# A pass that puts products of ones into TensorE's order where a replay of the plan sees it wait

## The chip, the cores and the metric

The kernel runs on one core of one Trainium2 chip. The metric is the device time of one execution in microseconds (us), as the median of several runs. The engines are named as in the profile: PE (TensorE, its products) and PEld (its weight loads), DVE (VectorE), ACT (ScalarE), POOL (GpSimd), SP (SyncE, which issues all transfers here).

## The reference

Two layers of a streaming encoder for 512 prompt positions and 64 sample positions, all in float32, width 1024:

```python
def trunk_layer(x, conv_state, k_past, v_past, ki_past, ...):
    a, g, q, k, v, qi, ki, wi = jnp.split(x @ w_in, points, axis=-1)
    u = a * jax.nn.sigmoid(g)
    conv_out, new_conv = conv_mixer(u, conv_state, conv_w, conv_b, cln_g, cln_b)   # 31 taps, layer norm, silu
    ...                                                                            # rope of q, k, qi, ki
    attn_out = dsa_attention(q, k_all, v_all, qi, ki_all, wi, pos, topk)           # indexer picks topk keys
    mix = jnp.concatenate([conv_out, attn_out], axis=-1) @ w_o
    x = layer_norm(ALPHA * x + mix, ln1_g, ln1_b)
    gate, up = jnp.split(x @ w_gate_up, 2, axis=-1)
    ffn = (jax.nn.silu(gate) * up) @ w_down
    x = layer_norm(ALPHA * x + ffn, ln2_g, ln2_b)
    return x, k, v, ki, new_conv
```

## The kernel before

Positions lie along the free dimension (576 columns, in two halves of 288), features on the 128 partitions. Each operand of the large products is split into a high and a low float32r part, and a product is made of three float32r products (`XH,whi`, `XH,wlo`, `XL,whi`). The small products (convolution, attention values, sums for the layer norms) are float32.

Nothing is issued while the program is being written down. Every call goes to a `Plan`, which records an operation with its views, its priority and a price per engine (`price`, from line 217). At the end `schedule` lays all operations out in time with those prices, engine by engine, by priority and readiness, with transfers and buffer places; the order that comes out is issued to the five queues by `issue` (line 352; all instructions carry line 362 for that reason). Each queue then runs strictly in that order on the chip, and what a wait really costs the plan does not know. Prices are, for instance, 0.069 us + n/960 for a DVE operation on n columns, 0.06 us + n/1200 (+ 0.035 outside PSUM) for ACT, 0.15 us + 0.0021 n for POOL.

The stages of a layer, twice over: the input products with rope and the indexer (to about 110 us of layer 1), the selection of keys on DVE and the convolution (64 x 5 products per layer, whose tap matrices `taps` POOL makes from `eyes` and `wv`), attention in blocks 0 to 4 (`logits` with products `qk`, `values` with transposes `pp` and products `po`), the convolution's layer norm (`conv_sums`, `Moments.stats`, `Moments.spread`), the output products, layer norm 1 (`Sums`), then the gated FFN in four parts as products of halves (`Seven`, products `q`, `r`, `c`) and the down products, layer norm 2.

One PSUM tile of two banks, tag `w` (function `wide`), is shared in turn by the convolution's accumulators (`conv`), `stats`, `spread`, `cshift` and the logits of attention block 4. It was shaped `[P, 2, 512]`. A convolution group is five products that accumulate in one stretch of its columns; the products of other work may stand between them in PE's order.

Of the kernel before, what the change touches and what calls it, by code (L numbers as in the profile page):

```python
# [11 lines left out]
F32 = mybir.dt.float32  # L12
F32R = mybir.dt.float32r
# [43 lines left out]
UW = PH * CIN  # L57
CWID = PH * COUT

O_CB, O_CG, O_CBE = 0, NCT * PH, NCT * PH + NCT  # L60
# [110 lines left out]
TABLES = {AF.Exp: "exp", AF.Silu: "silu", AF.Sigmoid: "sigmoid", AF.Sqrt: "sqrt"}  # L171
HOP, TABLE_LOAD, TABLE_LEAD = 0.2, 1.283, 0


class Plan:
# [77 lines left out]
    def schedule(self):  # L253
# [96 lines left out]
        return order  # L350

    def issue(self):
        nc = self.tc.nc
        take = lambda v: v.real() if isinstance(v, View) else v
        with self.tc.manual_schedule():
            for op in self.schedule():
                for t in op.tiles.values():
                    if t.ap is None:
                        tag = f"{t.tag}.{t.place}"
                        t.ap = t.pool.tile(t.shape, t.dt, tag=tag, name=t.name, bufs=1)  # L360
                engine = getattr(nc, op.done[2])
                getattr(engine, op.method)(*map(take, op.args), **{k: take(v) for k, v in op.kw.items()})  # L362
# [3 lines left out]
def stream_step(ctx, tc, ins, outs):  # L366
# [44 lines left out]
    def wide(name):  # L411
        return pw.tile([P, 2, 512], F32, tag="w", name=name)

# [75 lines left out]
    class Moments:  # L489
# [5 lines left out]
        def stats(self):  # L495
            m, tiles, count = self.m, self.tiles, self.count
            ps = wide("stats")
            for b, c in ((0, 496), (1, 504)):
                for i in range(tiles):
                    nc.tensor.matmul(ps[:m, 0, c + i:c + i + 1], self.s[b][:, i * m:(i + 1) * m], ones[:, 0:1],  # L500
                                     start=True, stop=True)
# [3 lines left out]
            nc.vector.tensor_scalar(nmu, ps[:m, 0, 496:496 + tiles], -1.0 / count, None, op0=OP.mult)  # L505
            nc.vector.tensor_mul(msq, nmu, nmu)
            nc.vector.scalar_tensor_tensor(rstd, ps[:m, 0, 504:504 + tiles], 1.0 / count, msq,
                                           op0=OP.mult, op1=OP.subtract)
            nc.vector.tensor_scalar(rstd, rstd, 0.0, LN_EPS, op0=OP.max, op1=OP.add)
            nc.scalar.activation(rstd, rstd, AF.Sqrt)  # L510
            nc.vector.reciprocal(rstd, rstd)

        def spread(self, b):

            m, tiles, n, dst = self.m, self.tiles, self.n, self.dst[b]
            per = tiles if tiles == 3 else tiles // 2
            ps = wide("spread")
            for i in range(tiles):
                nc.tensor.matmul(ps[:, i // per, (i % per) * m:(i % per + 1) * m],
                                 self.st[:m, b, i:i + 1].to_broadcast([m, P]), ident[:m, :m], start=True, stop=True)  # L520
# [122 lines left out]
    def layer(l):  # L643
# [10 lines left out]
        def convolve(c):  # L654
# [8 lines left out]
            for b in range(PH):  # L663
# [3 lines left out]
                                     wv[:, b, :].unsqueeze(2).to_broadcast(shape))  # L667
                o = b % 4 * COUT
                for j in range(CJ):
                    nc.tensor.matmul(ps[:, b // 4, o:o + COUT], sw[:, j * P:(j + 1) * P], v[:, b, j:j + COUT],  # L670
                                     start=(j == 0), stop=(j == CJ - 1))
            y = slot.tile([P, PH, COUT], F32, tag=f"u{c}", name=f"y{c}")
            for h in range(2):
                nc.vector.tensor_add(y[:, 4 * h:4 * h + 4, :], ps[:, h, :4 * COUT].rearrange("p (b t) -> p b t", b=4),
                                     prm[0][:, O_CB + c * PH + 4 * h:O_CB + c * PH + 4 * h + 4].unsqueeze(2)
# [11 lines left out]
        def conv_sums():  # L687
# [5 lines left out]
            for c in range(4):  # L693
                acc = cs[c]
                if c == 0:
                    shift = slot.tile([P, UW], F32, tag="u0", name="cshift")[:, :CWID]
                    ps = wide("cshift")
                    for h in range(2):
                        nc.tensor.matmul(ps[:, h, :CWID // 2], ones, acc[:, h * CWID // 2:(h + 1) * CWID // 2],
                                         start=True, stop=True)  # L700
# [213 lines left out]
        def logits(t, u):  # L914
# [13 lines left out]
            else:  # L928
                g = u // 2
                ps = wide("qk").rearrange("p a b -> p (a b)")  # L930
                q = qsm[:, u * P:(u + 1) * P]
# [395 lines left out]
```

## Time and profile before

| | |
|---|---|
| median of 3 runs | 1520.78 us (1516.83 to 1522.31) |
| the profiled execution: device time | 1524.12 us |
| its span from first to last instruction | 1522.4 us |
| its mean granted TensorE clock | 0.939 |
| busy: PE / DVE / ACT / POOL | 1449.1 / 1104.6 / 721.4 / 496.0 us |

All rows are from the one profiled execution. [...] A matmul's end is modelled, so PE can be called busy throughout a stretch in which its products merely follow each other more slowly; the spacing from start to start tells the real rate.

### The profile page before, as it was taken

The numbers are of one execution on the slowest core, as the hardware profiler recorded it, in microseconds if no ns is written. First come the engines' busy times: TensorE is split into PE (matmuls) and PEld (weight loads), VectorE is DVE, ScalarE is ACT, GpSimd is POOL, SyncE is SP. The second block draws the span as 40 slices with busy tenths as digits, with TensorE's granted clock in tenths as the row PEclk, the third lists the DMA queues.
The fourth block names the chain that finished last, engine by engine and source line by source line (L and its number), as shares of the span: only waits on it lengthen the run. The fifth ranks groups of instructions, "written<-read, shape, count | busy, mean of one in ns | idle before, by whom it ended". The sixth has DMA issues, their size and how long they took to land.

```text
span 1522.4 us, 26598 instructions
## 1 busy us (share of the span) xinstructions
PE 1449.1 (95%) x10246; PEld 1413.3 (93%) x10246; DVE 1104.6 (73%) x2040; ACT 721.4 (47%) x1421; POOL 496.0 (33%) x437
## 2 busy tenths in 40 slices
PE   6999999998999999999998998999899999999996
PEld 6889897997999999999998998889889999999996
DVE  3679886468678577587768997855596875865875
ACT  4444445645446245265444434465363552543643
POOL 2322554243113123033614245633420230320342
PEclk9989787898999999999999995959999999999997
DMA  5614220011222322223234241101112222222221
GB/s 201 188 52 119 54 70 17 29 56 56 77 104 78 103 89 92 84 98 103 69 102 125 86 125 52 45 14 42 56 50 88 99 94 87 94 91 81 80 74 63
DMA packets 66207, 125.12 MB, mean 82 GB/s; under 512 B 27936, under 2 KB 34208, under 8 KB 66080
## 3 DMA queue, kind: packets, MB, share of 16 engines
q1 hardware_dynamic: 66080, 123.42, 25.3%
q8 instruction: 80, 1.31, 0.4%
q14 instruction: 47, 0.39, 0.1%
HBM read 108.81 MB, written 9.21 MB: 78 GB/s over the span
## 4 chain that ended last, share of the span: by engine, by line
PE 78%; DVE 13%; ACT 3%; issue 2%; DMA 2%; POOL 1%; SPq 1%; ACTq 0%; DVEq 0%; POOLq 0%
PE prod L362 33%; PE q L362 16%; PE r L362 8%; PE conv L362 5%; PE c L362 4%; PE po L362 3%; DVE X L362 2%; DVE sel L362 2%; DVE rope_h L362 2%; PE qk L362 2%; PE dots L362 2%; PE pp L362 2%; PE spread L362 2%; DVE wlo L362 2%; PE stats L362 1%
## 5 line engine op out<-in xcount | busy, mean ns | idle before, releaser
L362 DVE TENSOR_TENSOR wlo<-raw,whi 128x512 fp32r<-128x512 f32 (+2 forms) x199 | 246.2, 1239 | 90.8 <-ACT whi L362 88.7
L362 ACT ACTIVATE whi<-raw 128x1024 fp32r<-128x1024 f32 (+2 forms) x206 | 182.9, 889 | 254.5 <-PE prod L362 179.1
L362 PE MATMUL prod<-XH,whi 128*128 128x288 f32 (+2 forms) x928 | 282.9, 310 | 18.5 <-ACT whi L362 16.4
L362 PE MATMUL prod<-XH,wlo 128*128 128x288 f32 (+2 forms) x928 | 285.0, 310 | 7.4 <-DVE wlo L362 7.4
L362 PE MATMUL prod<-XL,whi 128*128 128x288 f32 (+2 forms) x928 | 285.9, 310 | 2.9 <-DVE XL L362 2.8
L362 PE MATMUL prod<-hl,whi 128*128 128x288 f32 x704 | 208.1, 296 | 0.7 <-DVE hl L362 0.5
L362 PE MATMUL prod<-hh,wlo 128*128 128x288 f32 x704 | 207.8, 296 | 0.0
L362 PE MATMUL prod<-hh,whi 128*128 128x288 f32 x704 | 207.0, 295 | 0.0
L362 PEld LDWEIGHTS prod<-XH,whi 128*128 128x128 f32 (+1 forms) x928 | 177.6, 193 | 22.5 <-ACT whi L362 17.3
L362 PEld LDWEIGHTS prod<-XH,wlo 128*128 128x128 f32 (+1 forms) x928 | 177.9, 192 | 10.4 <-DVE wlo L362 8.3
L362 PEld LDWEIGHTS prod<-XL,whi 128*128 128x128 f32 (+1 forms) x928 | 178.9, 193 | 7.7 <-DVE XL L362 5.8
L362 ACT ACTIVATE whi<-s 128x512 fp32r<-128x512 f32 x160 | 96.4, 626 | 134.9 <-PE q L362 102.0
L362 DVE TENSOR_TENSOR wlo<-s,whi 128x512 fp32r<-128x512 f32 x158 | 107.7, 703 | 63.5 <-ACT whi L362 62.5
L362 PE MATMUL q<-XH,wlo 128*128 128x288 f32 x480 | 141.2, 296 | 1.5 <-DVE wlo L362 1.3
L362 PE MATMUL q<-XL,whi 128*128 128x288 f32 x480 | 141.4, 295 | 0.0
L362 PE MATMUL q<-XH,whi 128*128 128x288 f32 x480 | 141.3, 295 | 0.0
L362 PEld LDWEIGHTS prod<-hl,whi 128*128 128x128 f32 x704 | 132.1, 188 | 1.8 <-DVE hl L362 1.4
L362 PEld LDWEIGHTS prod<-hh,wlo 128*128 128x128 f32 x704 | 132.0, 188 | 0.1
L362 PEld LDWEIGHTS prod<-hh,whi 128*128 128x128 f32 x704 | 131.9, 188 | 0.2
L362 POOL TENSOR_TENSOR s<-raw 128x512 f32<-128x512 f32 x28 | 45.0, 1611 | 247.8 <-DVE wlo L362 209.7
L362 DVE TENSOR_TENSOR X<-X,prod 128x288 f32<-128x288 f32 x120 | 53.4, 451 | 86.8 <-PE prod L362 86.1
L362 POOL TENSOR_TENSOR taps<-eyes,wv 128x640 f32<-128x640 f32 x64 | 86.9, 1361 | 71.0 <-PE conv L362 57.2
(197 smaller groups left out, 3560.1 us busy)
## 6 DMA issues: line engine op xcount, KB each, us to landing
raw<-in_w_u SPq DMA_DIRECT2D x44, 512.0 KB, 3.2
raw<-in_w_g SPq DMA_DIRECT2D x44, 512.0 KB, 3.2
raw<-in_w_in SPq DMA_DIRECT2D x36, 512.0 KB, 3.9
raw<-in_w_d SPq DMA_DIRECT2D x48, 384.0 KB, 3.0
raw<-in_w_o SPq DMA_DIRECT2D x16, 512.0 KB, 3.3
raw<-in_w_d SPq DMA_DIRECT2D x16, 256.0 KB, 2.6
rope_s<-rope_h SPq DMA_DIRECT2D x48, 72.0 KB, 2.0
ud<-u SPq DMA_DIRECT2D x8, 320.0 KB, 2.9
```

The source lines that it names most:

```text
L362: getattr(engine, op.method)(*map(take, op.args), **{k: take(v) for k, v in op.kw.items()})
```

## The change

A new pass `filled` takes the order that `schedule` gave and replays it: five queues in order, the same prices with some corrections (a port that DVE and POOL hold in turn, a table load, transfers at 300 GB/s with 1.2 us at the end, `spacing` for the products, always at the full clock). Where the replay finds PE waiting by `t - now`, it puts `int(0.9 * wait / 0.237)` markers ahead of the waiting operation. `issue` turns a marker into a float32 product of the tile of ones with itself, 128 x 128 by 128 columns, into columns 816 to 943 of the `w` tile that was last opened, which nothing else uses. While an accumulation group of a `w` tile is open, markers are held back (`due`) until it is closed. For the first product the wait counts from 1.0 us on. The condition with `FORCE` never holds, since `FORCE` is 0.

The `w` tile becomes `[P, 1024]`, so that its columns can be cut as one range; for that, the copies out of the `spread` of the convolution's norm and out of `cshift` are two activations of 304 columns instead of one of 608. Everything else computes what it did.

```diff
+WB = CWID // 2
...
+SIGNAL, IDLE, FILL, CLOCK, FORCE, LATE = 0.04, (0.237, 0.213), 0.9, 3.4, 0.0, 1
...
+    def filled(self, order):
+
+        free, ended, held, out = dict.fromkeys(("tensor", "vector", "scalar", "gpsimd", "sync"), 0.0), {}, {}, []
+        dma, table, port, recent, act, begun = 0.0, None, ["", 0.0], [], 0.0, False
+        for op in order:
+            e = op.done[2]
+            t = free[e]
+            for w in op.waits:
+                if w.done[2] != e:
+                    t = max(t, ended[w.seq] + SIGNAL)
+                elif e != "tensor":
+                    t = max(t, ended[w.seq] + 0.02)
...
+            if op.method == "dma_start":
+                free[e] = t + op.generate
+                dma = max(dma, free[e] + 0.65) + op.nbytes / 300e3
+                end = dma + 1.2
+            elif e == "tensor":
+                cost, streamed = self.spacing(op)
+                now = free[e]
+                if not begun:
+                    now, begun = 1.0, True
+                n = int(FILL * (t - now) / IDLE[0])
+                while recent and recent[0][0] < now - CLOCK:
+                    act -= recent.pop(0)[1]
+                if act < FORCE * CLOCK and n < LATE:
+                    n += 1
+                for _ in range(n):
+                    out.append(None)
+                    recent.append((now, IDLE[1]))
+                    act += IDLE[1]
+                    now += IDLE[0]
+                t = max(t, now)
+                recent.append((t, streamed))
+                act += streamed
+                free[e] = t + cost
+                end = free[e] + 0.18
...
+    def spacing(self, op):
+
+        n = op.args[0].columns()
+        if op.method == "transpose":
+            return 0.111, n / 2400
+        if n == 1:
+            return 0.16, 0.0
+        if F32R in (op.args[1].tile.dt, op.args[2].tile.dt):
+            return max(0.111, 0.0065 + 0.0004375 * n), n / 2400
+        return 2 * max(0.111, 0.0065 + 0.000875 * n), n / 600
+
     def issue(self):
         nc = self.tc.nc
         take = lambda v: v.real() if isinstance(v, View) else v
         with self.tc.manual_schedule():
-            for op in self.schedule():
+            t, cols, ones = self.filler
+            idle, due, group = t.pool.tile(t.shape, t.dt, tag=f"{t.tag}.0", name=t.name, bufs=1), 0, set()
+            for op in self.filled(self.schedule()):
+                if op is None:
+                    due += 1
+                while due and not group:
+                    nc.tensor.matmul(idle[:, cols], take(ones), take(ones), start=True, stop=True)
+                    due -= 1
+                if op is None:
+                    continue
+                if op.method == "matmul" and op.args[0].tile.tag == self.filler[0].tag:
+                    (group.discard if op.kw["stop"] else group.add)(op.args[0].idx.flat[0])
...
     def wide(name):
-        return pw.tile([P, 2, 512], F32, tag="w", name=name)
+        return pw.tile([P, 1024], F32, tag="w", name=name)
...
     nc.gpsimd.memset(ones, 1.0)
+    nc.filler = Held(pw.pool, [P, 1024], F32, "w", "idle", 1), slice(512 + WB, 512 + WB + P), ones
...
-            if tiles > per:
-                nc.scalar.activation(dst.rearrange("p (a b) -> p a b", a=2), ps[:, :, :n // 2], AF.Copy)
-            else:
-                nc.scalar.activation(dst, ps[:, 0, :n], AF.Copy)
+                o = 512 * (i // per) + i % per * m
+                nc.tensor.matmul(ps[:, o:o + m], self.st[:m, b, i:i + 1].to_broadcast([m, P]), ident[:m, :m], start=True, stop=True)
+            for a in range(0, n, per * m):
+                nc.scalar.activation(dst[:, a:a + per * m], ps[:, a // (per * m) * 512:][:, :per * m], AF.Copy)
...
-                    nc.scalar.activation(shift.rearrange("p (a b) -> p a b", a=2), ps[:, :, :CWID // 2], AF.Copy,
-                                         scale=-1.0 / P)
+                    for h in range(2):
+                        nc.scalar.activation(shift[:, h * WB:(h + 1) * WB], ps[:, 512 * h:512 * h + WB], AF.Copy,
+                                             scale=-1.0 / P)
```

## Rows read from the trace of the kernel before

**Rows 1.** From the page: busy time of each engine, and the granted clock of TensorE in 40 equal slices (9 is 0.9 or more).

```profile
PE 1449.1 (95%) x10246; PEld 1413.3 (93%) x10246; DVE 1104.6 (73%) x2040; ACT 721.4 (47%) x1421; POOL 496.0 (33%) x437
...
PEclk9989787898999999999999995959999999999997
```

**Rows 2.** The windows view, all engines: stretch (us from the start of the span) and its length; then busy us and number of instructions of PE, PEld, DVE, ACT and POOL; then the granted clock, the DMA share and GB/s.

```profile
76.00:79.00 3.00, 1.00 (x9) 0.99 (x10) 2.77 (x6) 0.32 (x1) 0.63 (x1) 1.00 0.05 10
79.00:89.40 10.40, 10.40 (x49) 10.40 (x49) 6.00 (x10) 2.29 (x6) 5.46 (x4) 0.51 0.01 3
166.00:171.30 5.30, 2.67 (x23) 2.54 (x22) 5.21 (x14) 3.00 (x5) 2.58 (x3) 1.00 0.35 113
171.30:198.50 27.20, 26.64 (x122) 25.64 (x123) 19.81 (x53) 11.87 (x37) 16.28 (x17) 0.50 0.15 42
199.00:238.00 39.00, 37.91 (x313) 35.65 (x313) 34.88 (x87) 16.67 (x45) 20.43 (x17) 1.00 0.21 56
238.00:246.90 8.90, 6.63 (x42) 4.62 (x41) 8.63 (x18) 5.91 (x14) 7.50 (x6) 0.97 0.08 17
246.90:277.00 30.10, 29.21 (x138) 27.31 (x139) 12.89 (x26) 18.39 (x30) 11.38 (x8) 0.50 0.05 18
340.00:348.00 8.00, 3.97 (x24) 3.41 (x24) 7.31 (x17) 6.70 (x16) 4.97 (x4) 0.84 0.09 31
348.00:358.20 10.20, 10.20 (x48) 10.20 (x49) 5.42 (x12) 1.03 (x3) 2.72 (x2) 0.50 0.22 80
909.00:917.00 8.00, 4.53 (x36) 4.41 (x34) 7.60 (x16) 3.85 (x7) 5.29 (x5) 0.90 0.29 93
916.50:946.50 30.00, 28.01 (x132) 26.80 (x132) 23.42 (x56) 13.04 (x40) 14.52 (x15) 0.51 0.15 45
979.00:985.00 6.00, 4.72 (x29) 3.98 (x29) 5.75 (x12) 3.11 (x7) 3.94 (x3) 0.89 0.34 92
983.50:1018.00 34.50, 33.54 (x155) 31.05 (x156) 20.40 (x40) 17.57 (x34) 15.85 (x11) 0.51 0.03 7
1089.00:1097.50 8.50, 3.92 (x27) 3.49 (x26) 7.80 (x16) 6.43 (x15) 5.74 (x5) 0.93 0.16 61
1097.50:1108.00 10.50, 10.50 (x54) 10.50 (x54) 5.73 (x15) 1.69 (x5) 1.96 (x1) 0.57 0.14 51
1506.00:1522.40 16.40, 5.39 (x24) 4.77 (x24) 8.31 (x23) 5.76 (x12) 0.86 (x2) 0.50 0.26 89
```

**Rows 3.** The timeline of PE, for the spacing (start to start) of the same kinds of product at either level of the clock.

```profile
87.17 0.44 PE L362 MATMUL prod<-XH,whi 128*128 128x288 f32 x1
87.41 0.44 PE L362 MATMUL prod<-XL,whi 128*128 128x288 f32 x1
...
199.87 1.24 PE L362 MATMUL conv<-v,taps 128*128 128x76 f32 x10
200.94 0.60 PE L362 MATMUL po<-vt,pt 128*128 128x64 f32 x4
```

**Rows 4.** The timeline of PE at two of its long waits: start us, us, instruction, how many merged, and in square brackets the idle time before it with its releaser. One product of the program with float32 operands appears as two records here (640 conv records stand for 2 x 4 x 8 x 5 products).

```profile
167.60 1.06 PE L362 MATMUL conv<-v,taps 128*128 128x76 f32 x8
171.31 0.66 PE L362 MATMUL qk<-k,q 128*128 128x128 f32 x2 [2.64 <-DVE mx L362]
171.76 0.65 PE L362 MATMUL conv<-v,taps 128*128 128x76 f32 x2
...
911.32 1.51 PE L362 MATMUL conv<-v,taps 128*128 128x76 f32 x12
916.30 0.66 PE L362 MATMUL qk<-k,q 128*128 128x128 f32 x2 [3.48 <-DVE mx L362]
916.76 1.93 PE L362 MATMUL conv<-v,taps 128*128 128x76 f32 x8
...
919.55 2.25 PE L362 MATMUL conv<-v,taps 128*128 128x76 f32 x10
921.54 0.67 PE L362 MATMUL qk<-k,q 128*128 128x128 f32 x2
```

**Rows 5.** The timeline of PE at its first products.

```profile
14.01 0.61 PE L362 MATMUL prod<-XH,whi 128*128 128x288 f32 x1 [14.01 <-ACT whi L362]
...
14.66 0.44 PE L362 MATMUL prod<-XH,whi 128*128 128x288 f32 x1
14.90 0.44 PE L362 MATMUL prod<-XL,whi 128*128 128x288 f32 x1
...
17.79 0.29 PE L362 MATMUL prod<-XL,whi 128*128 128x288 f32 x1
17.92 0.29 PE L362 MATMUL prod<-XH,wlo 128*128 128x288 f32 x1
```

**Rows 6.** The waits view of PE: who waited for whom; us in total, number of times, the longest in us.

```profile
PE qk L362 <- DVE mx L362: 8.9, 5, 3.5
...
PE stats L362 <- DVE s L362: 6.0, 4, 4.2
```

**Rows 7.** Groups by form of DVE and ACT (out<-in, shapes, count | busy us, mean ns | idle before with releasers), and one row of the DMA view (count, KB each, median us from issue to landing).

```profile
L362 DVE TENSOR_TENSOR wlo<-raw,whi 128x1024 fp32r<-128x1024 f32 x95 | 139.9, 1473 | 40.4 <-ACT whi L362 39.8
...
L362 ACT ACTIVATE whi<-raw 128x1024 fp32r<-128x1024 f32 x100 | 105.8, 1059 | 94.5 <-PE prod L362 66.0 <-DMA raw<-in_w_in 15.1 <-PE c L362 6.2
...
raw<-in_w_in SPq DMA_DIRECT2D x36, 512.0 KB, 3.9
```

More of the change, by code (lines that the diff above doesn't have):

```diff
@@ L350, in schedule @@
         return order
+    def filled(self, order):
[9 more added lines that the diff above has]
+                    t = max(t, ended[w.seq] + 0.02)
+            for x in op.tiles.values():
+                last = held.get((id(x.pool), x.tag, x.place))
+                if last and last[0] is not x:
+                    t = max(t, last[1] + SIGNAL)
+            if op.method == "dma_start":
[22 more added lines that the diff above has]
+                end = free[e] + 0.18
+            else:
+                cost = op.cost[e]
+                if e == "scalar":
+                    if op.table not in (None, table):
+                        t += TABLE_LOAD
+                        table = op.table
+                    free[e] = t + cost
+                    end = free[e] + 0.1
+                else:
+                    x = t
+                    if e == "gpsimd" and op.method != "memset" or e == "vector" and self.two_read(op):
+                        if port[0] != e:
+                            x = max(x, port[1])
+                        port[:] = e, x + cost
+                    free[e] = x + cost
+                    end = free[e] + 0.09
+            out.append(op)
+            ended[op.seq] = end
+            for x in op.tiles.values():
+                key = (id(x.pool), x.tag, x.place)
+                last = held.get(key)
+                held[key] = x, max(end, last[1]) if last and last[0] is x else end
+        return out
@@ new lines, in two_read @@
+    def two_read(self, op):
+        return (op.method in ("tensor_add", "tensor_sub", "tensor_mul", "scalar_tensor_tensor")
+                and not any(v.tile.pool is p for v in op.args if isinstance(v, View) for p in self.psum))
+    def spacing(self, op):
[7 more added lines that the diff above has]
+        return 2 * max(0.111, 0.0065 + 0.000875 * n), n / 600
@@ L360, in issue @@
                         t.ap = t.pool.tile(t.shape, t.dt, tag=tag, name=t.name, bufs=1)
+                        if t.tag == self.filler[0].tag:
+                            idle = t.ap
                 engine = getattr(nc, op.done[2])
@@ L499, in stats @@
                 for i in range(tiles):
-                    nc.tensor.matmul(ps[:m, 0, c + i:c + i + 1], self.s[b][:, i * m:(i + 1) * m], ones[:, 0:1],
+                    nc.tensor.matmul(ps[:m, c + i:c + i + 1], self.s[b][:, i * m:(i + 1) * m], ones[:, 0:1],
                                      start=True, stop=True)
@@ L667, in convolve @@
                                      wv[:, b, :].unsqueeze(2).to_broadcast(shape))
-                o = b % 4 * COUT
+                o = b // 4 * 512 + b % 4 * COUT
                 for j in range(CJ):
-                    nc.tensor.matmul(ps[:, b // 4, o:o + COUT], sw[:, j * P:(j + 1) * P], v[:, b, j:j + COUT],
+                    nc.tensor.matmul(ps[:, o:o + COUT], sw[:, j * P:(j + 1) * P], v[:, b, j:j + COUT],
                                      start=(j == 0), stop=(j == CJ - 1))
@@ L698, in conv_sums @@
                     for h in range(2):
-                        nc.tensor.matmul(ps[:, h, :CWID // 2], ones, acc[:, h * CWID // 2:(h + 1) * CWID // 2],
+                        nc.tensor.matmul(ps[:, 512 * h:512 * h + WB], ones, acc[:, h * CWID // 2:(h + 1) * CWID // 2],
                                          start=True, stop=True)
-                    nc.scalar.activation(shift.rearrange("p (a b) -> p a b", a=2), ps[:, :, :CWID // 2], AF.Copy,
-                                         scale=-1.0 / P)
+                    for h in range(2):
+                        nc.scalar.activation(shift[:, h * WB:(h + 1) * WB], ps[:, 512 * h:512 * h + WB], AF.Copy,
+                                             scale=-1.0 / P)
                 eng = nc.vector if c == 3 else nc.gpsimd
@@ L929, in logits @@
                 g = u // 2
-                ps = wide("qk").rearrange("p a b -> p (a b)")
+                ps = wide("qk")
                 q = qsm[:, u * P:(u + 1) * P]
```

8 lines of the change are left out of this document (3 added, 5 removed).

## The prediction

> **What bounds the kernel now.** I read the page first [rows 1]: PE is called busy for 1449.1 of 1522.4 us, no other engine comes near, and the row of granted clocks shows slices well below 9. So there are two things to win on PE: its 73.3 us without work, and the time in which it works at half speed. The windows view [rows 2] was read next, in pairs: a stretch in which PE has gaps, and the one behind it. The reader is to see that each stretch at about 0.50 follows one in which PE was busy for much less than its length (1.00 of 3.00 us, 2.67 of 5.30, 6.63 of 8.90, 3.97 of 8.00, 4.53 of 8.00, 4.72 of 6.00, 3.92 of 8.50), and that in the slow stretch PE is then busy nearly throughout (26.64 of 27.20 us, 29.21 of 30.10). The stretch 199 to 238, with the same kinds of small products and PE busy for 37.91 of 39.00 us, stays at 1.00. So gaps come first, the lower clock follows, and then PE is the engine that the others wait for. The timeline [rows 3] gives the price: conv products follow each other every 0.199 us at half speed ((921.54 - 919.55)/10, [rows 4]) and every 0.107 us at full speed ((200.94 - 199.87)/10); prod goes from 0.24 us (87.41 - 87.17) to 0.13 us (17.92 - 17.79, [rows 5]). PE at full speed needs about 0.55 of its time at half speed. The long runs of nines in the page's clock row, the FFN above all, have nothing to give back.
>
> The first products tell the same, and that the profile's row can mislead: they are 0.24 us apart at 14.66 and 0.13 us apart at 17.79 [rows 5], although the page's clock row starts with a 9 [rows 1]. After 14 us without work PE starts at the lower level. [...]
>
> **What the change adds.** One idle product is a float32 product by 128 columns, two records. The trace has none. Its bounds are two conv records of 76 columns, 0.214 us, and two prod records of 288 columns, 0.264 us, at full speed, and 0.40 to 0.48 us at half speed; I take the middle, 0.24 and 0.43 us. In a gap of PE it costs nothing: the waiting for DVE or ACT covers it. Where PE doesn't wait, it moves all that PE does behind it.
>
> How many? The pass divides 0.9 of a wait by 0.237 us. PE's idle time is 73.3 us, of which 14.0 are the start [rows 5] and 16.4 - 5.4 = 11.0 the end [rows 2]; the other 48 give some 183 products. In the slow stretches the replay, which knows only the full clock, sees further waits: PE's 148 us in the seven of them before the end become 82, while DVE, ACT and PE set 99 (next part), so 17 us or some 65 products. For the start I follow the pass by hand: eight transfers of X and cos and sin at 0.98 us each, two small ones, and one weight of 1.75 us end at about 14.3 us, the split by ACT at 15.4, so int(0.9 x 14.4 / 0.237) = 54 products. In all some 300, or 600 records.
>
> **The start.** On the chip the 54 products begin at about 1 us at half speed; 14.01 to 17.60 were slow before [rows 5], so about 3.6 us of that again, which is 8 products, and the 46 others take 46 x 0.237 = 10.9 us: they end at 15.5 us, where the first real product began at 14.01. That one is 1.5 us late. Against it, the 14 products that ran at 0.24 us then run at 0.13: 14 x 0.11 = 1.5 us back. Sum 0; bounds -1.5 and +1.5 us.
>
> **What the slow stretches give back** [rows 2]. The new length of each is at least what PE at 0.55, DVE or ACT needs, whichever is most:
> 79 to 89.4: DVE 6.0 of 10.4, at most 4.4 us; 171.3 to 198.5: DVE 19.8 of 27.2, 7.4; 246.9 to 277: ACT 18.4 of 30.1, 11.7; 348 to 358.2: PE 5.6 of 10.2, 4.6; 916.5 to 946.5: DVE 23.4 of 30.0, 6.6; 983.5 to 1018: DVE 20.4 of 34.5, 14.1; 1097.5 to 1108: PE 5.8 of 10.5, 4.7; the end from 1506: 0.45 x 5.39 = 2.4. Together 55.9 us. A few shorter slow spells I give nothing.
>
> How much of each is taken? In 246.9 to 277 and 983.5 to 1018 the products of attention alternate with ACT and the convolution's norm is one chain of sums, DVE, ACT and products; what is late next there is the latency of that chain, which no clock shortens. I take half of 25.8, 12.9 us. In the two around the layer norms I also take half, 4.6 of 9.3. In 79 to 89.4, where plain prods and conv run with nothing waiting for them soon, 0.6 of 4.4, 2.6. At the end, where `stats` and `spread` lie on the path themselves and stand behind a wait of 4.2 us for DVE [rows 6], 1.5 of 2.4.
>
> In 171.3 to 198.5 and 916.5 to 946.5 I take only a quarter, 3.5 of 14.0, for a reason that is in the order itself. The waits that come ahead of these, 2.64 and 3.48 us for DVE's `mx` [rows 4], stand behind 8 and 12 records of conv. A group is ten records, so both times a group is open (8 of 10; 10 and 2 of the next 10), and `issue` holds the markers back: they come out behind the wait, after the 2 or 8 records that close the group. The gap stays empty, the clock falls as before, and the products of ones then lift it again.
>
> Gain: 12.9 + 4.6 + 2.6 + 1.5 + 3.5 = 25.1 us.
>
> **What it costs.** Products where nothing waits: 0 if the replay errs only towards too few. It should err that way mostly: its price of a DVE split of 1024 columns is 0.069 + 1024/960 = 1.14 us where the chip needs 1.473, and of ACT's 0.95 where the chip needs 1.059 [rows 7], so it sees DVE and ACT done too early and waits too short. Only its transfers are dear: 512 KB by 0.65 + 1.75 + 1.2 us besides the issue's 0.63, 4.2 us, where the median is 3.9 [rows 7]. The upper bound is the slow rival below, 31 us. I take one product in twenty, 15 x 0.24 = 3.6 us, near the lower end because of those prices. The two halves of six copies cost a second fixed part, about 0.2 us (1.059 less 1024/1200) each; three a layer are on the norm's chain, but the first half starts four products earlier: 0 to 1.2, taken 0.6. The order of `schedule` may shift a little with these added operations; I reckon nothing.
>
> **The sum.** -25.1 + 3.6 + 0.6 + 0 = -20.9 us. The profiled execution took 1524.1 us, which makes 1503.2; it was 3.3 us above the median of the runs, so the forecast is 1500 us.
>
> **The rivals.**
> *Too little is filled.* The replay's DVE is faster than the chip's by the rows above, and four of the seven gaps before slow stretches lie where DVE is busy nearly throughout (2.77 of 3.00, 5.21 of 5.30, 8.63 of 8.90, 7.60 of 8.00). If the replay has DVE done in time there, no product is put in. Then the long chains of the norms and the end alone gain, 2.3 + 1.5, less 0.6: about 1518 us. Against it: DVE and POOL hold the port in turn in the replay, which lengthens its DVE.
> *The attention stretches stay slow.* Busyness alone doesn't raise the clock there (29.21 of 30.10 us at 0.50), and their products are short, transposes among them. Without their 12.9 us, and with 17 products more at 0.43 us, 7.3 us, of the gain 0.7 us is left: 1520 us. [...] Against it: 199 to 238 has the same mixture and stays at 1.00.
> *Everything holds.* Three quarters of 55.9 with the same costs of some 2 us: -40, 1481 us.
> *Held-back products, slower than before.* In the two convolution stretches PE has no slack at half speed. The 10 and 13 products of the two waits come out behind them, and the replay sees further waits of 19.8 - 14.7 = 5.1 and 23.4 - 15.4 = 8.0 us there, 19 and 30 products. If the clock does not come back, all 72 run at 0.43 us on the path, 31.0 us, against 21.6 from the other stretches less 0.6: +10, or 1531 us by the median. It decides from the point where over 50 of these products run at the lower clock. Against it: each slow stretch of [rows 2] did end, behind work without gaps. That the products hold the clock nowhere, so that the change doesn't do what it says, gives no other time and is counted here.
>
> **How the numbers follow.** Forecast 0.48, from 1486 to 1513; everything holds 0.10; too little 0.19; attention slow 0.07; slower 0.16. A measurement of this kernel can tell about 0.5%, 7.6 us, from no change. Faster by more than that: 0.48 + 0.10 + 0.03 of too little = 0.61. Within it: 0.16 + 0.07 = 0.23. Slower: 0.16. The range leaves out the slower case and the far end of everything holds, 0.19 in all: 1472 to 1526 us.
>
> **What would show it.** Some 600 records of ones by ones, about 108 of them before the first prod. The granted clock at 1.00 in the layer norms' stretches and at the end, mostly 1.00 in 246.9 to 277 and its twin, still at 0.50 for a few us behind the two `mx` waits with the products of ones on the far side of conv; mean clock near 0.98. Gaps of PE filled, but the FFN stretches as long as before. Wrong if products of ones stand by the dozen in the FFN or the input products while PE had no gap there, if the clock falls behind filled gaps, or if the stretches keep their length at full clock because ACT or DVE set it.

## The result and the profile after

The changed kernel takes 1538.01 us (median of 4 runs, 1526.79 to 1543.32) where the kernel before took 1519.17 beside it: ratio 1.0129, 95% interval 1.0098 to 1.016. It is slower by about 19 us where I forecast 20 us less. The profiled execution took 1543.32 us, with a mean granted clock of 0.967 against 0.939. Medians are over all runs, while a ratio leaves out runs over 1.5% above the fastest of their kernel, so the two can differ by a few tenths of a percent (e8 below: 1524.17/1517.8 = 1.0042 by median, 1.0017 as ratio).

So the mean clock rose, as it was meant to, and the time went the other way. From the page of after (compare [rows 1]): PE is busy 53.6 us longer. The clock row still has a 7 and an 8 at its seventh and eighth slices (231 to 308 us), an 8 at the 22nd and a 7 at the 27th (1002 to 1041 us). One operation has gone from POOL to DVE: 436 and 2041 instructions, where before had 437 and 2040.

```profile
PE 1502.7 (97%) x11054; PEld 1471.6 (95%) x11054; DVE 1098.4 (71%) x2041; ACT 721.4 (47%) x1427; POOL 490.6 (32%) x436
...
PEclk9999997899999999999998999979999999999998
```

The rows of lines for the products of ones hold 300 + 222 + 118 + 96 + 58 + 14 = 808 records, 404 products; I had counted some 300. The first row gives the tile into which most went (`spread`: the layer norms' `w` tile), then records, duration in ns and first and last start.

```profile
L447 PE MATMUL spread<-ones x300: 270/275/580, 353.5 to 1530.9; 128*128 128x128 f32 x150
...
L447 PE MATMUL conv<-ones x222: 271/275/530, 77.1 to 961.4; 128*128 128x128 f32 x111
...
L447 PE MATMUL idle<-ones x118: 270/275/579, 1.0 to 68.2; 128*128 128x128 f32 x118
```

To find where the time went, each product of the program was sought in both traces, and its start in one was taken from its start in the other. The table gives how much this offset grows in a stretch (us, times of the kernel before). It is one execution against one, and two columns tell what that can show. e9 has before's order and no product of ones, and differs by up to 1.6 us, but in 960 to 1070 by 6.3. In 55 to 130, e3 differs by 3.8 us without a product there. So these two stretches are not read, and in the others what is over 4 us, or comes back in each kernel that has the products.

| stretch | what | after | e1 no products | e3 attention only | e5 old order | e9 no products, old order | e11 mended | e12 bad ones only |
|---|---|---|---|---|---|---|---|---|
| 55 to 130 | start of conv | -0.6 | +0.3 | -3.8 | -0.1 | +0.3 | -4.7 | -0.2 |
| 160 to 215 | conv 1 | +1.8 | +1.2 | +0.8 | +0.1 | 0.0 | -2.9 | -0.2 |
| 233 to 300 | attention 3, 4 and conv norm, layer 1 | +9.5 | +3.7 | +8.1 | -5.9 | 0.0 | -6.4 | -1.3 |
| 330 to 390 | layer norm 1 | -2.3 | -0.3 | +0.3 | -2.4 | 0.0 | -1.8 | -0.1 |
| 722 to 785 | layer norm 2 of layer 1 | +5.4 | 0.0 | 0.0 | +5.4 | 0.0 | 0.0 | +5.4 |
| 785 to 880 | start of layer 2 | +7.2 | +1.0 | +0.9 | +4.3 | -0.9 | +0.7 | +5.9 |
| 900 to 960 | conv 2 | -4.4 | -2.0 | -4.2 | -2.8 | -1.6 | -3.3 | -0.7 |
| 960 to 1070 | attention and conv norm, layer 2 | +2.5 | -0.5 | +2.5 | -2.6 | -6.3 | -1.9 | -3.4 |
| 1070 to 1150 | layer norm 1, layer 2 | -2.5 | -0.2 | -0.2 | -2.5 | -0.7 | -2.5 | -0.9 |
| from 1490 | last norm | +2.2 | 0.0 | 0.0 | +2.6 | 0.0 | +0.3 | +1.7 |

In after, the FFN stretches (390 to 722, 1150 to 1490) are as long as before, within 0.1 us. The loss of after has three places: 233 to 300, 722 to 785 and 785 to 880.

**The stretches of [rows 2] in the trace of after.** The same work stands up to 21 us later in after, so each window here runs between the same products as in before; columns as there. In order: the first attention stretch (246.9 to 277 in before), layer norm 1 (340 to 358.2), the second convolution (916.5 to 946.5), the second attention stretch (983.5 to 1018), layer norm 1 of layer 2 (1089 to 1108), the end (from 1506). The layer norms 1 are at 1.00 throughout and 2.0 and 2.5 us shorter, the second convolution is at 0.94. Both attention stretches are still slow for a good part: 0.59, and 6.5 us longer than in before, and 0.74. The end is at 0.61.

```profile
252.30:288.90 36.60, 35.56 (x186) 33.80 (x185) 12.65 (x25) 22.87 (x38) 10.24 (x9) 0.59 0.04 15
351.00:367.20 16.20, 15.63 (x130) 15.21 (x130) 12.98 (x29) 7.72 (x19) 7.72 (x5) 1.00 0.19 66
936.90:963.50 26.60, 24.91 (x198) 23.80 (x198) 21.18 (x56) 13.02 (x41) 13.97 (x16) 0.94 0.17 50
1000.50:1033.40 32.90, 29.61 (x179) 26.47 (x179) 23.30 (x42) 19.39 (x36) 15.11 (x10) 0.74 0.03 7
1108.50:1125.00 16.50, 15.95 (x133) 15.52 (x133) 13.29 (x29) 7.97 (x19) 7.70 (x5) 1.00 0.18 65
1524.40:1541.50 17.10, 6.92 (x38) 5.62 (x37) 8.31 (x23) 5.75 (x12) 0.86 (x2) 0.61 0.25 86
```

**Layer norm 2 of layer 1: products where nothing waited.** Timeline of PE, first in before, then the same place in after. In before, `stats` begins with no idle time, the first product of layer 2 after 0.87 us and the one of `XL` after 0.23. In after, 24, 14 and 16 records of ones stand ahead of those three. The 24 alone take 757.99 - 755.09 = 2.90 us, where nothing was to be covered.

```profile
746.20 0.29 PE L362 MATMUL prod<-hh,whi 128*128 128x288 f32 x1
746.37 0.64 PE L362 MATMUL stats<-ones,s 128*96 128x1 f32 x6
...
755.72 0.67 PE L362 MATMUL prod<-XH,whi 128*128 128x288 f32 x3 [0.87 <-ACT XH L362]
756.62 0.40 PE L362 MATMUL prod<-XL,whi 128*128 128x288 f32 x1 [0.23 <-DVE XL L362]
```

```profile
754.97 0.29 PE L460 MATMUL prod<-hh,whi 128*128 128x288 f32 x1
755.09 2.84 PE L447 MATMUL spread<-ones 128*128 128x128 f32 x24
757.99 0.67 PE L460 MATMUL stats<-ones,s 128*96 128x1 f32 x6
...
766.35 1.72 PE L447 MATMUL spread<-ones 128*128 128x128 f32 x14
767.83 0.64 PE L460 MATMUL prod<-XH,whi 128*128 128x288 f32 x3
768.31 1.95 PE L447 MATMUL spread<-ones 128*128 128x128 f32 x16
770.01 0.38 PE L460 MATMUL prod<-XL,whi 128*128 128x288 f32 x1
```

At the start of layer 2 the products stand in the wrong places too: the longest real wait behind the first product, 4.33 us for `wtok` (2.60 in before), holds none, the input products that follow run at half speed (838.40 to 838.64: 0.24 us for a product) as behind that wait in before (819.55 to 819.79: 0.24), and 16 records stand at 841.97 where before had no gap.

```profile
830.54 0.27 PE L460 MATMUL wtr<-ident,wt 8*128 8x8 f32 x1 [4.33 <-DVE wtok L460]
...
838.40 0.44 PE L460 MATMUL prod<-XL,whi 128*128 128x288 f32 x1
838.64 0.44 PE L460 MATMUL prod<-XH,wlo 128*128 128x288 f32 x1
...
841.97 2.10 PE L447 MATMUL conv<-ones 128*128 128x128 f32 x16
```

**233 to 300: DVE's order is another one.** Timeline of DVE in before, then in after. `prob` is the softmax's operation that yields `mx`, for which `qk` waits on PE. In before, a `prob` stands between the 1.58 us `sel` and `c<-c,cshift`, and the next one starts 2.47 us after the latter. In after, `c<-c,cshift` (here 1.96 us) and a `sel` of 1.61 us follow each other, and both `prob` come behind.

```profile
241.44 1.58 DVE L362 TENSOR_SCALAR sel<-sel 64x576 f32<-64x576 f32 x1
243.05 0.69 DVE L362 CUSTOM_DVE_ANT_0 prob<-qk,bias 128x512 f32<-128x512 f32 x1
...
243.66 1.34 DVE L362 TENSOR_TENSOR c<-c,cshift 128x608 f32<-128x608 f32 x1
...
246.13 0.69 DVE L362 CUSTOM_DVE_ANT_0 prob<-qk,bias 128x512 f32<-128x512 f32 x1
```

```profile
244.61 1.96 DVE L460 TENSOR_TENSOR c<-c,cshift 128x608 f32<-128x608 f32 x1
246.59 1.61 DVE L460 TENSOR_SCALAR sel<-sel 64x576 f32<-64x576 f32 x1
248.23 0.69 DVE L460 CUSTOM_DVE_ANT_0 prob<-qk,bias 128x512 f32<-128x512 f32 x1
...
248.85 0.69 DVE L460 CUSTOM_DVE_ANT_0 prob<-qk,bias 128x512 f32<-128x512 f32 x1
```

What PE makes of it, in its timeline: in before, the logits product `qk` waits 1.03 us for its `mx`. In after, three products of ones (6 records) stand ahead of the same `qk`, and then comes a wait of 3.19 us that the replay did not see. Behind it `po` follows at half speed (8 records in 1.59 us; the clock is 0.50 in 249 to 252), and at 278.35 sixteen products of ones, 5.73 us of them on the way to the last logits. The third fence is e10 below, a kernel without any product of ones whose `cshift` copies are split: it has the long wait too (3.59 us), and e1 has it with 3.92.

```profile
243.80 0.74 PE L362 MATMUL qk<-k,q 128*128 128x512 f32 x2 [1.03 <-DVE mx L362]
```

```profile
244.96 0.83 PE L447 MATMUL cshift<-ones 128*128 128x128 f32 x6
248.99 1.22 PE L460 MATMUL qk<-k,q 128*128 128x512 f32 x2 [3.19 <-DVE mx L460]
250.01 1.80 PE L460 MATMUL po<-vt,pt 128*128 128x64 f32 x8
251.60 1.06 PE L460 MATMUL pp<-ident,prob 128*128 128x128 f32 x4
...
278.35 5.67 PE L447 MATMUL qk<-ones 128*128 128x128 f32 x32
284.08 0.50 PE L460 MATMUL qk<-kp,qsm 128*128 128x512 f32 x1
```

```profile
248.90 1.22 PE L477 MATMUL qk<-k,q 128*128 128x512 f32 x2 [3.59 <-DVE mx L477]
```

### The profile page after: what moved, and what is told of

It is laid out like the page before. It is cut to its first block, busy times and chain, and to the rows that moved or that the text cites. A ratio compares the mean times of both kernels' runs of the same rounds, so it can differ in the third digit from the quotient of the medians.

```text
span 1541.5 us, 28222 instructions
## 1 busy us (share of the span) xinstructions
PE 1502.7 (97%) x11054; PEld 1471.6 (95%) x11054; DVE 1098.4 (71%) x2041; ACT 721.4 (47%) x1427; POOL 490.6 (32%) x436
## 4 chain that ended last, share of the span: by engine, by line
PE 83%; DVE 10%; DMA 2%; ACT 2%; issue 1%; POOL 1%; SPq 0%; ACTq 0%; DVEq 0%; POOLq 0%
PE prod L460 34%; PE q L460 17%; PE r L460 8%; PE conv L460 4%; PE c L460 4%; PE po L460 3%; PE dots L460 2%; DVE X L460 2%; DVE rope_h L460 2%; PE conv L447 2%; DVE sel L460 2%; PE qk L460 2%; PE spread L460 1%; PE pp L460 1%; DMA raw<-in_w_in 1%
## 5 line engine op out<-in xcount | busy, mean ns | idle before, releaser
L460 PE MATMUL prod<-XL,whi 128*128 128x288 f32 (+2 forms) x928 | 280.3, 304 | 0.0
L460 PE MATMUL prod<-XH,wlo 128*128 128x288 f32 (+2 forms) x928 | 279.7, 303 | 0.0
L460 PE MATMUL prod<-XH,whi 128*128 128x288 f32 (+2 forms) x928 | 277.4, 304 | 0.2
L460 PEld LDWEIGHTS prod<-XL,whi 128*128 128x128 f32 (+1 forms) x928 | 173.6, 187 | 2.9 <-DVE XL L460 0.9
L460 PEld LDWEIGHTS prod<-XH,whi 128*128 128x128 f32 (+1 forms) x928 | 172.1, 187 | 3.3 <-ACT whi L460 0.9
L460 PEld LDWEIGHTS prod<-XH,wlo 128*128 128x128 f32 (+1 forms) x928 | 173.3, 187 | 1.9
```

## Two theories and the experiments

Theory A: the loss is products of ones that stand where PE does not wait, because the replay invents waits. Theory B: it is the plan's order, which the added copies shift. Neither excludes the other, so the question is what each is worth. Each kernel was timed beside the kernel before (medians 1515.6 for e1 to e4, 1517.8 for e5 to e8, 1516.2 for e9 to e12); ratios are to it, with their 95% interval.

**e1, the change without its products.** Only the tile's shape, the split copies and the order that they bring are left. All kernels of this first group use one filter, which drops markers by the position of the product of PE behind them:

```diff
+KEPT = ()
...
+    def kept(self, order):
+        out, k, n = [], 0, 0
+        for op in order:
+            if op is None:
+                n += 1
+                continue
+            if op.done[2] == "tensor":
+                if any(a <= k < b for a, b in KEPT):
+                    out += [None] * n
+                n, k = 0, k + 1
+            out.append(op)
+        return out
...
-            for op in self.filled(self.schedule()):
+            for op in self.kept(self.filled(self.schedule())):
```

> The changed kernel with its pass, tile shape, split copies and order, but all 404 products of ones left out. Theory A (the loss is products of ones that stand where the chip does not wait): within 0.4% of the kernel before, 1513 to 1526 us, granted clock near 0.94. Theory B (the split copies shift the plan's order, and that shift is the loss, above all around the convolution's norm of layer 1 where DVE's mx came 3.2 us late): slower by 6 us or more, 1526 us and up, with the stretch around 240 to 285 us longer by 5 us.

1526.33 us, 1.0063 (1.0034 to 1.0092), just within what B expected. Without any product of ones the change costs 0.6%. B has a share; the rest, 1.0129 against 1.0063, is the products' in that order.

**e2, e3, e4, a third of the products each**: 118 in the layer norms 1, at the start of the FFN and the last norm; 144 in convolution, attention and convolution's norm; 142 at the start of both layers and in layer norm 2 of layer 1.

```diff
-KEPT = ()
+KEPT = ((1813, 2300), (6256, 7100), (9038, 9560))   # e2
+KEPT = ((969, 1350), (5748, 6130))                  # e3
+KEPT = ((0, 480), (4261, 5252))                     # e4
```

> Only the 118 products around the layer norms 1, the start of the FFN, and the last layer norm. By the offsets between the two traces these stages moved -2.4, -2.5 and +2.1 us. Theory A: 2.8 us faster than the run without products (about -0.2%), gaps of 3.55 us before the first late product of each norm filled and the clock at 1.00 there. Theory B: the same difference, on a slower base.

> Only the 144 products in the convolution, attention and the convolution's norm of both layers. The offsets of these stages were +1.8, +9.5, -4.4 and +2.5 us. Theory A: 9 us slower than the run without products, most of it from the 16 and 20 products ahead of the second logits product of attention block 4. Theory B: no more than 3 us slower than that run, since the late mx is there without products too.

> Only the 142 products at the start of either layer and around layer norm 2 of layer 1. The offsets were +0.2, -0.5, +5.2 and +7.4 us. Theory A: 10 to 12 us slower than the run without products. Theory B: the part at the start of layer 2 (+7.4, of which 1.7 us is a longer wait for DVE that holds no product) is there without products, so no more than 6 us slower.

e2: 1523.40, 1.0052 (1.002 to 1.0083). e3: 1530.03, 1.0091 (1.0066 to 1.0117). e4: 1542.00, 1.0184 (1.0111 to 1.0256; 4 runs, hence the wide interval). Against e1's 1.0063, only e4's interval lies apart: the products at the starts and in layer norm 2 cost, for the others the intervals overlap e1's, so neither the norms' nor attention's products show a gain in this order. Against e1's median, within the noise for the first two, that is -2.9 us for e2, as expected, +3.7 for e3, near B's 3 and not A's 9, and +15.7 for e4, more than A's 10 to 12. The table's 233 to 300 shows why for e3: +8.1 us, with the same wait of 3.19 us and the same 32 late records as in after.

**e5, the old order with the products.** The kernel before (tile of two banks, whole copies) and the pass as it is, 395 products; the queues other than PE's are before's.

```diff
-                    nc.tensor.matmul(idle[:, cols], take(ones), take(ones), start=True, stop=True)
+                    nc.tensor.matmul(idle[:, 1, cols], take(ones), take(ones), start=True, stop=True)
...
-    nc.filler = Held(pw.pool, [P, 1024], F32, "w", "idle", 1), slice(512 + WB, 512 + WB + P), ones
+    nc.filler = Held(pw.pool, [P, 2, 512], F32, "w", "idle", 1), slice(WB, WB + P), ones
...
```

> The kernel before, with its tile shape, single copies and order untouched, plus the pass: 395 products of ones. Takes the share of the split copies and the shifted order (0.6% in the run without products) out. Theory A (products that stand where nothing waits make the rest): slower than before by 0.4 to 1.0%, 1521 to 1531 us, with late PE again around layer norm 2 (+5 us) and at the start of layer 2 (+7 us). Theory B (order alone): no slower than before.

1521.47, 1.0022 (0.9981 to 1.0062), clock 0.985. The change less its new order does not differ from before by more than the noise. In 233 to 300 the same pass now gains 5.9 us; its windows there (columns as in [rows 2]; up to 233 us e5 runs in step with before, within 0.1 us) are at 1.00 throughout:

```profile
240.00:250.00 10.00, 8.48 (x72) 7.33 (x71) 8.47 (x16) 6.53 (x16) 5.90 (x4) 1.00 0.01 2
250.00:260.00 10.00, 9.93 (x91) 9.42 (x91) 5.52 (x14) 7.19 (x12) 3.85 (x3) 1.00 0.00 0
260.00:270.00 10.00, 7.88 (x59) 6.75 (x59) 4.91 (x8) 7.91 (x11) 5.95 (x5) 1.00 0.09 31
```

In layer norm 2, the start of layer 2 and the last norm it loses what after loses, or nearly (5.4, 4.3 and 2.6 us), and gives the gain back.

**e6 and e8, the replay without the port.** The condition by which the replay has DVE and POOL hold its port in turn is taken out, in after (e6, 188 products) and in e5 (e8, 185).

```diff
                     if e == "gpsimd" and op.method != "memset" or e == "vector" and self.two_read(op):
-                        if port[0] != e:
-                            x = max(x, port[1])
                         port[:] = e, x + cost
```

> The changed kernel, but its replay lets DVE and POOL work at the same time (no turn on the port): 188 products instead of 404; of the 12 + 7 + 8 ahead of layer norm 2 and the 25 at the start of layer 2 four are left. If the turn on the port is what invents the waits: 10 us faster than the changed kernel, about 1522 to 1528 us, level with the run without products or a little below it. If the false waits come from the transfers or the DVE prices: no more than 4 us faster than the changed kernel.

> The kernel before with its own order, plus the pass without the turn on the port: 185 products, mostly at the start, in the layer norms 1, at the end and ahead of the output products. Theory A: faster than before by 3 to 8 us, 1508 to 1513 us, the norms' stretches at full clock. If filled gaps are worth nothing because the chain of DVE and ACT sets these stretches: within 2 us of before.

e6: 1526.39, 1.0079 (1.0054 to 1.0104), 0.5% below after by ratio (though the ends of the two intervals, 1.0104 and 1.0098, just overlap) and 11.6 us by median, as theory A has it: with the port gone, more than half of all products are gone, layer norm 2 adds 0.5 us in place of 5.4 and the start of layer 2 adds 0.7. But that is e1 again, not better. e8: 1524.17, 1.0017 (0.9971 to 1.0063), where a gain was expected: a miss. With the invented waits the replay lost real ones: in 240 to 270 e8's clock is 0.87, 0.50 and 0.50 where e5's is 1.00, and the stretch adds 2.4 us. Leaving the port out is not the remedy.

**e7, the price of one.** e1 with 100 products put evenly into the FFN of layer 1, where PE has next to no gap (in before it is idle for 1.4 us of 390 to 722).

```diff
+                if k in range(2300, 4200, 19):
+                    out.append(None)
```

> The run without products, plus 100 products of ones at even distances in the FFN of layer 1, where PE has no gap: the price of one that is in the way. Theory A: 100 x 0.22 to 0.24 us, 22 to 24 us slower than the run without products, about 1550 us. If such a product hides in the weight loads or costs more around it: below 12 or above 30 us.

1546.38, 1.0173 (1.0107 to 1.0238). Against e1 that is (1546.38 - 1526.33)/100 = 0.20 us each, a little under the 0.22 to 0.24 expected; in the one trace, the offset between the first and the last of them grows by 21.6 us, 0.22 each. So most of the 0.24 us that one takes in the row of 24 records above (2.90/12) comes on top.

**e9 and e10, which copy shifts the order.** Both without products. e9 splits the copies out of `spread` and leaves `cshift`'s whole, as below; e10 is the reverse, `spread`'s copies whole and `cshift`'s split.

```diff
-                    for h in range(2):
-                        nc.scalar.activation(shift[:, h * WB:(h + 1) * WB], ps[:, 512 * h:512 * h + WB], AF.Copy,
-                                             scale=-1.0 / P)
+                    nc.scalar.activation(shift.rearrange("p (a b) -> p a b", a=2),
+                                         ps.rearrange("p (a b) -> p a b", a=2)[:, :, :WB], AF.Copy, scale=-1.0 / P)
```

> No products of ones; the flat tile shape and the two copies behind spread split, the copy behind cshift left whole. Laid out by the plan, every queue has exactly the order of the kernel before (the split copies apart). Theory B, now: the order is the loss without products, the split copies themselves cost nothing: within 0.3% of before. If the split copies or the flat shape cost by themselves: about +0.6%, as the run without products.

> No products of ones; only the copy behind cshift split in two, the copies behind spread whole. Laid out by the plan, 599 places of DVE's queue and 300 of PE's differ from before, from the first convolution norm on. Theory B: +0.6%, 1524 to 1528 us, like the run without products; otherwise as before.

e9: 1516.03, 1.0003 (0.9978 to 1.0028). e10: 1522.68, 1.0048 (1.0027 to 1.0069). Splitting `spread` leaves all queues in before's order; splitting `cshift` moves 599 places of DVE's queue and 300 of PE's, and takes the addition `c<-c,cnmu` of one layer from POOL to DVE. Two activations more on ACT, an engine that is busy for 721.4 of 1522.4 us in before, come with 0.5%. That the order does it, and not the halves of `cshift` themselves, is argued from e9, where four more activations cost nothing, and from the wait for `mx` above; split `cshift` copies in before's order were not run.

**e11, mended.** The old order (all copies whole) and the pass's products less those at the start, in layer norm 2, at the start of layer 2 and ahead of the second logits of block 4; 14 in place of 22 in each layer norm 1; and where a group is open, they go ahead of it and so into the gap, not behind it. 195 are left.

```diff
+KEPT = {378: 7, 969: 10, 1813: 14, 5748: 13, 6590: 14, 9542: 14}
+KEPT.update({k: None for a, b in ((980, 1345), (1349, 1350), (1817, 2300), (5756, 6122), (6126, 6130), (6594, 7100), (9548, 9560))
+             for k in range(a, b)})
...
+            if op.done[2] == "tensor":
+                n = min(n, KEPT[k] or n) if k in KEPT else 0
+                if not opened:
+                    at = len(out)
+                out[at:at] = [None] * n
```

> All copies whole, so the order of the kernel before; 195 of the pass's products kept: none at the start, around layer norm 2, at the start of layer 2 and ahead of the second logits product of attention block 4; 14 instead of 22 ahead of the late product of each layer norm 1; those that an open convolution group held back are put ahead of that group. If the prediction's gains are there once order and misplaced products are out: -1.0 to -1.6% against before. If the slow stretches give nothing back at full clock: within 0.4%.

1503.89 (1495.51 to 1518.62), **0.9914** (0.9882 to 0.9945): faster than both, and a little short of the 1.0% that was the least expected, which its interval reaches. With fewer than half of after's products the clock is 0.977, above after's 0.967. Two windows of it: the first is the convolution stretch behind a `mx` wait (171.3 to 198.5 in before, at 0.50), the second the second half of layer norm 1 (348 to 358.2, at 0.50). With 14 products in place of 22 ahead of it, that one is not at 1.00 as in after, and the stretch 330 to 390 gains 1.8 us where after gains 2.3.

```profile
166.80:190.10 23.30, 20.18 (x159) 18.85 (x160) 21.81 (x53) 11.60 (x37) 17.19 (x17) 0.97 0.13 37
334.20:343.10 8.90, 8.43 (x58) 8.12 (x59) 5.78 (x13) 1.03 (x3) 2.85 (x2) 0.81 0.27 101
```

**e12, the bad ones alone.** The old order and only the 90 products of layer norm 2, the start of layer 2 and the last norm.

```diff
+KEPT = ((4261, 5252), (9038, 9560))
```

> All copies whole, so the order of the kernel before; only the 90 products around layer norm 2 of layer 1, at the start of layer 2 and ahead of the last norm. By the offsets of the trace of the run in the old order (+5.4, +4.3, +2.6 us): +0.7 to +0.9%. If they only shift waits about: within 0.3%.

1531.32, 1.0107 (1.0062 to 1.0151), above the 0.7 to 0.9% expected, which its interval holds: these products alone, most of which e11 leaves out, cost 1.1%. 90 products at e7's 0.20 to 0.22 are 18 to 20 us; measured 1531.32 - 1516.2 = 15.1.

## Why the prediction was wrong

**The start: right.** 54 products were forecast, ending at 15.5 with nothing won or lost. There are 108 records from 1.00 us, the first real product stands at 15.42, and the offset is +0.2 us at 55, where kernels without a product there differ by -0.5 to +1.2.

```profile
1.00 14.66 PE L447 MATMUL idle<-ones 128*128 128x128 f32 x108 [1.00 <-POOL ones L460]
15.42 0.38 PE L460 MATMUL prod<-XH,whi 128*128 128x288 f32 x1
```

**That products of ones hold the clock: right, but for the end.** The forecast took it for granted that a product which nobody reads serves as well as a real one; no trace of before shows it, and it was my assumption. The runs do: against 0.939 in before, e5 has 0.985 and e11 0.977, and behind the filled gaps of the layer norms 1 after is at 1.00 where before is at 0.50 and 0.57.

**The gain of the attention stretches, 12.9 us for the two: the first right in the order of before and wrong in the change, the second not shown.** Half of 11.7, 5.9 us, was taken for the first; e5 shows -5.9 and e11 -6.4, after +9.5. The gain was worked out on the rows of before, and the change no longer had that order. The rival that this stretch stays slow, with transposes among its products, falls with e5's windows at 1.00, in which products of ones stand among the transposes; in after its outcome came about all the same, by the longer wait. For the second I took half of 14.1. But the same stretch in e9, with no product of ones, takes 28.4 us at 0.79 where the profiled execution of before has 34.5 at 0.51: part of what I counted as gain is a difference between executions, and -2.6 in e5 and -1.9 in e11 show none beyond it.

**The layer norms, 4.6 us: right** (2.3 + 2.5 in after). **The split copies, 0.6 us:** as a cost of their own nothing that can be measured (e9, 1.0003). **The end, 1.5 us: wrong in sign**; after loses 2.2 us there and e12, where only the last norm's products stand at the end, 1.7. Of the 25 products there, five stand ahead of a `stats` that did not wait in before, and the clock of the end is still 0.61 in after; e11, with 17 of them, is at +0.3. **79 to 89.4, 2.6 us:** open, since the stretch differs by more than that without a product.

**The convolutions, a quarter of 14.0:** the held-back products stand where forecast, 15 of them behind the wait:

```profile
171.01 0.66 PE L460 MATMUL qk<-k,q 128*128 128x128 f32 x2 [2.66 <-DVE mx L460]
171.47 0.65 PE L460 MATMUL conv<-v,taps 128*128 128x76 f32 x2
171.91 5.79 PE L447 MATMUL conv<-ones 128*128 128x128 f32 x30
177.46 0.42 PE L460 MATMUL qk<-k,q 128*128 128x128 f32 x2
```

They cost 177.46 - 171.91 = 5.55 us there, after which the clock is back (0.58 in 172.0 to 177.5, 1.00 in 177.5 to 190); over the two stretches after is at +1.8 and -4.4. So the slow rival, which put 31.0 us on just these products, saw the mechanism, and it is not where the loss lies.

**The first step that failed:** "The order of `schedule` may shift a little with these added operations; I reckon nothing." The added operations were worth 0.48% (e10) to 0.63% (e1), 7 to 10 us: a planner that ranks by priority and readiness gives a different order for two more operations, and here one in which `qk` waits 3.19 us for `mx`, where it waited 1.03.

**The second:** "I take one product in twenty, 15 x 0.24 = 3.6 us, near the lower end because of those prices." It measured 1.07% (e12), some 16 us. The price of one was nearly right (0.20 by e7); the number was not, and the reason was wrong with it. I argued from prices: DVE's split costs 1.14 us in the replay and 1.473 on the chip, so the replay sees DVE done too early and puts in too few. But 1.473 is a mean that holds waits for POOL. Of the 95 splits in the trace of before, 41 begin within a two-operand operation of POOL and take what is left of that plus 1.08 us; the other 54 take 1.19 to 1.24 (an example of either is in the last section). So the price of 1.14 is about what the operation itself takes, and the replay adds the wait for the port on top. It errs by the port, the other way: with it 404 products, without it 188, and of the latter only two stand in the three clusters of layer norm 2 shown, where after has 27. The code shows how it can invent a wait, though no run tested that apart: `port` keeps only its last holder, in the order of the plan and not of time, so an operation ready early waits for one that was listed ahead of it and itself waits for something late. I had named the port as an argument against the rival of too few products, and did not carry it into the cost. The sum of the waits gives the replay away: 404 products stand for at least 404 x 0.237 / 0.9 = 106 us of waits, where PE was without work for 73.3 us in before and the prediction found 17 more at the full clock.

**The sum.** In ratios: order +0.6% (e1), bad products +1.1% (e12), the good ones -0.9% (e11), together +0.8% where the whole change measures +1.29%. The intervals of the three leave room for the difference, and the three do not add up to the change: e11 moves the held-back products, and neither e11 nor e12 has those at the start or the 16 and 20 ahead of the second logits of block 4. The trace suggests where a further part may lie, in 233 to 300: without products +3.7 (e1), in the old order with them -5.9 (e5), and both together +9.5, as +8.1 in e3. Behind the new wait the clock is low (0.50 in 252.3 to 278.3 of after), and the sixteen late products run for the most part at half speed (0.65 over their 5.73 us). That both are needed there is seen in four single traces; that it makes up the rest of the 1.29% is not shown.

## What to carry to other kernels

Products of ones paid here in gaps that the measured trace shows, ahead of a wait (e11, -0.9%), and cost 0.20 to 0.22 us each where there was none (e7); a replay on the planner's prices is a list of candidates, and the list should be held against the trace before it is issued. When a change touches an operation that a planner orders, compare the queues with and without it before anything else: two copies in place of one, for each layer's `cshift`, cost 0.5% here with no work added on the engine that sets the end. A mean duration can hold waits for another engine (1.473 us here, where a split that did not wait took 1.19 to 1.24): look at single operations before calling a price too low. And e11 shows that fewer, placed by the trace, beat more: 195 products gain 0.9%, 395 in the same order nothing.

## What the runs showed of the hardware that was not expected

**DVE and POOL do hold each other up.** Timeline of POOL in before, then of DVE. POOL's first addition ends at 739.02 + 0.83 = 739.85. DVE's split of 1024 columns, with two operands, stands at 739.46 and takes 1.47 us: 0.39 to the end of that addition and 1.08 more. At 764.38, with no addition of POOL beside it, it takes 1.22. The other way round, the addition that starts within DVE's split takes 1.80 us and ends 0.7 us after it; those around it take 0.80 to 0.83.

```profile
739.02 0.83 POOL L362 TENSOR_TENSOR s<-s,sq 128x288 f32<-128x288 f32 x1
739.79 1.80 POOL L362 TENSOR_TENSOR s<-s,X 128x288 f32<-128x288 f32 x1
741.56 0.80 POOL L362 TENSOR_TENSOR s<-s,sq 128x288 f32<-128x288 f32 x1
```

```profile
739.46 1.47 DVE L362 TENSOR_TENSOR wlo<-raw,whi 128x1024 fp32r<-128x1024 f32 x1 [0.94 <-ACT whi L362]
...
764.38 1.22 DVE L362 TENSOR_TENSOR wlo<-raw,whi 128x1024 fp32r<-128x1024 f32 x1
```

The whole trace of before has it so nearly throughout: 41 splits begin within a two-operand operation of POOL and end 1.08 to 1.09 us behind it, and the additions of POOL on 288 columns that begin within such a split end 0.66 to 0.67 us behind that. Only two splits, at 344.90 and 1093.63, begin 0.64 us within an addition and still take 1.23, and there it is the addition that is long, 2.53 us. The replay was thus right to let either engine wait for the other; what it lacks, as its code reads, is which of the two started first.

**The granted clock alone did not tell the time.** After has a higher mean clock than before (0.967 against 0.939) and is 1.3% slower; e5 has the highest, 0.985, and is no faster than before.
